# A hybrid attention step on one core: the successor operand loaded by a job, read-backs on another queue, states loaded at another place

## The chip, the core and the metric

The program runs on one core of a Trainium2 chip. TensorE (PE in the profile) multiplies, ScalarE (ACT) and VectorE (DVE) evacuate and transform, GpSimd (POOL) selects and issues DMAs, SyncE (SP) issues DMAs only. Each engine works through its own instructions in order; an instruction that waits holds up all that stand behind it on its engine, and that holds for DMA issues too. SP, ACT and POOL each have such a DMA queue here. The metric is the device time of one execution in microseconds: 2400.34 us is the median of three runs of the kernel before (2395.4 to 2400.91).

## What is computed

One layer of a hybrid streaming encoder for 1024 prompt frames and 8 x 16 sample frames, width 2048, in float32. Cut to what matters:

```python
h = rms_norm(x, norm_pre)
q_sb,k_sb,v_sb,g_sb, q_r,k_r,v_r,g_r = split(h @ w_in)      # 8 blocks of 8 heads x 128
# branch A: stick-breaking attention, strictly causal; sample rows also see 1024 cached keys and values
z = q k^T / sqrt(128);  a = sigmoid(z) * cumprod of sigmoid(-z) over the later keys;  o_sb = a v
# branch B: retention with a decay per head; the state s of 128 x 128 runs over the frames
o_r = (q k^T * decay) v + (q s) * decay;   s = s * decay + k^T v
y = concat(head_rms_norm(o_sb) * silu(g_sb), head_rms_norm(o_r) * silu(g_r)) @ w_out
x = x + rms_norm(y, norm_post)
```

It also returns the new keys and values, and the retention states of the prompt and of the eight sample streams.

## The kernel before, in words

**Tiling.** Frames are cut into tiles of 128. There are two groups: group 0 has the prompt tiles 0 to 3 and the sample tile (640 columns), group 1 the prompt tiles 4 to 7 (512 columns). The normalised, transposed input of a group is the moving operand `mov`: 16 strips (k = 0 to 15) of 128 rows in four blocks of four, each strip split into a high part `mh` (a rounded copy, ScalarE, line 131) and a low part `ml` (the rest, VectorE, line 132). Every product is then three matmuls, high by high, high by low and low by high. There is one set of SBUF blocks for `mov`; group 1 takes the place of group 0 block by block, once the products that read a block are issued.

**Loops.** For each group and each of 8 heads the kernel projects six columns of w_in (`project`, line 243: q, k and gate of both branches; four chunks of weights, each a DMA `wr`, line 215, a split into `wh` and `wl`, and the matmuls of line 229), and for each pair of heads the two value columns (`project_rows`, DMA line 271, matmuls line 288, tile names `wrn`, `whn`, `wln`, `accn`). Weight tiles `wr`, `wh`, `wl` have four buffers each.

**Jobs.** Around these products run jobs, Python generators stepped by `tick()`, which is called once after each product; a job that yields n comes again n ticks later. Jobs are the two branches of a head (`ret_branch`, `sb_branch`) and in group 0 the decoding of the sample tile (`decode`). The numbers after the yields (D_RET, D_TO, D_TI and so on, one for group 0 and one for group 1) place their instructions among the products. A planner then gives each engine its order by its own estimate of when things are ready. `tied` holds an instruction, in group 0, behind the product issued last; it orders the plan and adds no wait on the chip.

**Turning a tile.** A 128 x 128 transpose is done by writing the tile to DRAM (`turn_out`, line 471), reading it back with 32 x 32 blocks rearranged (`turn_in`, line 477: four DMAs, line 481), and transposing the blocks on VectorE. The reading back goes to the SP queue for the retention keys (`ro<-s_rk`), for the outputs of both branches (`ro<-s_o`, `so<-s_o`, `do<-s_o`) and for the decoder's weights (`be<-s_bd`); only the attention weights of the prompt (`kb<-s_be`, `be<-s_be`) are read back on GpSimd's queue.

**The change of groups.** The last head of group 0 (h = 7) ends with `project_pair` (line 249), which works on two gate columns together. `load_moving` (line 198) runs along with it: four strips of group 1 at each of its chunks 1, 2 and 3, and the last four in the first `project_rows` of group 1. A strip is a DMA `mr<-s_h` on SP's queue into one of two buffers, and the split. The prompt keys of group 1's first attention, `kpast` (line 962), use the same two buffers afterwards.

**Other loads touched.** `keys_out` stores the new keys (`out<-kn`, lines 869 and 874) from ScalarE's queue: 4 DMAs per head, and 4 more where the sample tile is in the group. `sample_retention` (line 802) loads the eight stored states of a head in four DMAs (`st<-state_ret`, line 808, SP) right where it starts, at the end of the head's retention. `retention` (line 747) begins with the decay table `dT` (line 749, SP).

Of the kernel before, what the change touches and what calls it, by code (L numbers as in the profile page):

```python
# [9 lines left out]
F32 = mybir.dt.float32  # L10
# [6 lines left out]
P = 128  # L17
D = 2048
KT = D // P
# [29 lines left out]
D_TI = (32, 13)  # L49
D_OUT = 4  # L50
D_KL = 29
D_TK = 4
D_FIN = 4
D_MR = 6
# [6 lines left out]
def tile_hybrid_step(  # L61
# [136 lines left out]
    def load_moving(mov, at, n, src, stage=None):  # L198
        hi, lo = mov
        for k in range(KT):  # L200
# [7 lines left out]
            split(hi[q][:, j, at : at + n], lo[q][:, j, at : at + n], r)  # L208
            yield D_MR

    def load_w(col):
        hs, ls = [], []
        for w in range(KT // WQ):
            wr = wp.tile([P, WQ, P], F32, name="wr", tag="wr")
            nc.sync.dma_start(
                wr,
                w_in[0, w * WQ * P : (w + 1) * WQ * P, col : col + P].rearrange("(k p) e -> p k e", p=P),
            )
# [30 lines left out]
    def project_pair(g, mov, cols, loads=None):  # L249

        accs = [acc_banks(g) for _ in cols]
        chunks = [load_w(c) for c in cols]
        for w in range(KT // WQ):
            for i, (acc, chunk) in enumerate(zip(accs, chunks)):
                _, wh, wl = next(chunk)
                for _ in range(WQ if loads and w and i == 0 else 0):
                    next(loads)
                products(mov, acc, g["pieces"], w, wh, wl)
        return [list(zip(acc, g["pieces"])) for acc in accs]

    col = lambda i, h: i * H * P + h * P

    def project_rows(g, mov, col, dst, off, loads=None):
        hi, lo = mov
        nt = len(g["tiles"])
        banks = [
            accp.tile([P, 2, 2 * P], F32, name=f"accn{b}", tag=f"acc{b % 2}") for b in range((nt + 1) // 2)
        ]
        for w in range(KT // 2):
            wr = wp.tile([P, 2, 2 * P], F32, name="wrn", tag="wr")  # L270
            nc.sync.dma_start(
                wr,
                w_in[0, 2 * w * P : 2 * (w + 1) * P, col : col + 2 * P].rearrange("(k p) e -> p k e", p=P),
            )
            for _ in range(WQ if loads and w == 0 else 0):
                next(loads)
            wh = wp.tile([P, 2, 2 * P], F32R, name="whn", tag="wh")
            wl = wp.tile([P, 2, 2 * P], F32R, name="wln", tag="wl")
            split(wh, wl, wr)
            for j in range(2):  # L280
                q, jj = divmod(2 * w + j, WQ)
                for t in range(nt):
                    a = banks[t // 2][:, t % 2, :]
                    ts = slice(t * P, (t + 1) * P)
                    for n, (lhs, rhs) in enumerate(((hi, wh), (hi, wl), (lo, wh))):


                        anchor[0] = nc.tensor.matmul(  # L288
                            a,
                            lhs[q][:, jj, ts],  # L290
                            rhs[:, j, :],
                            start=(w == 0 and j == 0 and n == 0 and t % 2 == 0),
                            stop=(w == KT // 2 - 1 and j == 1 and n == 2 and (t % 2 == 1 or t == nt - 1)),
                        )
                    tick()
        for b, bank in enumerate(banks):
            m = min(2, nt - 2 * b)
            nc.scalar.activation(
                dst[:, off + 2 * b : off + 2 * b + m].rearrange("p t j d -> p t (j d)"), bank[:, :m, :], AF.Copy
            )  # L300

    with ExitStack() as s1:
# [171 lines left out]
            q.dma_start(s.rearrange("k q c -> q k c"), src)  # L474
            return s

        def turn_in(s, raw, q):

            for i in range(4):
                tied(  # L480
                    q.dma_start(  # L481
                        raw[32 * i : 32 * i + 32, :].rearrange("p (k a) -> p k a", a=32),
                        s[:, :, 32 * i : 32 * i + 32].rearrange("k (j b) a -> b (k j) a", b=32),
                    )
                )
# [44 lines left out]
        class Out:  # L530
# [9 lines left out]
            def finish(self, b, h, gT, oT, dst):  # L540
# [4 lines left out]
                s = turn_out(self.o, f"s_o{b}_{h}_{self.nt}_{phase[0]}")  # L545
                yield D_TO[phase[0]]
                flat = self.o.rearrange("p k d -> p (k d)")
                turn_in(s, flat, nc.sync)
                yield D_TI[phase[0]]
                n = self.nt * P  # L550
                tied(nc.vector.transpose(oT[:, :n], flat))
# [73 lines left out]
        def decode(h, qs, rest):  # L625
# [81 lines left out]
            for _ in range(2):  # L707
                values.append(load_v(len(values)))
                yield D_TO[phase[0]] // 2
            turn_in(turned, be, nc.sync)  # L710
            for _ in range(V_BUFS - 4):
                values.append(load_v(len(values)))
                yield D_TI[phase[0]] // 2
# [33 lines left out]
        def retention(gi, g, h, out, rq, rk, rkn, rv):  # L747
# [8 lines left out]
                nc.vector.tensor_tensor(sc, ps[:, :P], dT[:, kind, :], ALU.mult)  # L756
                return sc

            S = None
            if gi == 1:  # L760
                S = op.tile([P, P], F32, name="S", tag="S", bufs=3)
                nc.sync.dma_start(S, s_S[h])
# [34 lines left out]
                yield D_RET[phase[0]]  # L797
            nc.scalar.dma_start(s_S[h] if gi == 0 else s_prompt[0, 0, h], S)
            if SAMPLE in g["tiles"]:
                yield from sample_retention(h, out, sc, rq, rkn, rv)  # L800

        def sample_retention(h, out, sc, rq, rkn, rv):
            i = 4

            sts = []
            for c in range(4):
                st = ip.tile([P, 2, P], F32, name="st", tag="st", bufs=4)
                tied(nc.sync.dma_start(st, state_ret[0, 2 * c : 2 * c + 2, h].rearrange("b d e -> d b e")))
                sts.append(st)
            yield 2 * D_RET[phase[0]]  # L810
            po = acc_tile()
            nc.tensor.matmul(po[:, 2 * P : 3 * P], sc, rv[:, i, :], start=True, stop=True)
# [28 lines left out]
        def ret_branch(gi, g, h, rq, rk, rv, rest):  # L841
# [19 lines left out]
        def sb_branch(gi, g, h, out, q2, k2, kT, rest):  # L861
            tiles, nt = g["tiles"], len(g["tiles"])
            off = 0 if gi == 0 else 4
            def keys_out():
                kn = ep.tile([P, nt * P], F32, name="kn", tag="rkn")
                nc.vector.transpose(kn, kT[:, : nt * P])
                for i in range(4):
                    q, ds = slice(32 * i, 32 * i + 32), slice(32 * i, 32 * i + 32)
                    nc.scalar.dma_start(
                        k_prompt[0, 0, tiles[0] * P : (tiles[0] + 4) * P, h, ds].rearrange("(j b) a -> b j a", b=32),  # L870
                        kn[q, : 4 * P].rearrange("p (j a) -> p j a", a=32),
                    )
                    if SAMPLE in tiles:
                        nc.scalar.dma_start(
                            k_sample[0].rearrange("b t h d -> (b t) h d")[:, h, ds].rearrange("(j b) a -> b j a", b=32),
                            kn[q, 4 * P :].rearrange("p (j a) -> p j a", a=32),
                        )
                yield 1
# [16 lines left out]
        for gi, g in enumerate(GROUPS):  # L895
# [7 lines left out]
            for h in range(H):  # L903
# [328 lines left out]
```

## Time and profile before

| | |
|---|---|
| median of three runs | 2400.34 us |
| the profiled execution | 2397.79 us |
| its span, first to last instruction | 2396.1 us |
| mean granted TensorE clock | 0.993 |
| group 0 | to about 1120 us |
| change of groups | about 1080 to 1230 us |
| group 1 | from about 1130 to about 2000 us |
| output projection | from about 1963 us |

The profile is one execution on the chip. Its page gives busy time by engine, the chain of work that ended last, and the costliest groups; other views give the busy time of each engine in chosen stretches, who waited for whom, one tile's instructions, and the instructions in order of time. A line such as `L215` is a line of the kernel before; `wr<-w_in` names output and input tile. `SPq` and `ACTq` are DMA issues on those queues, with the time that the issue took, not the transfer. PEclk is the clock that TensorE was granted, as a share of the full one. What stands in square brackets at the end of a timeline row is the engine's idle time before the instruction, and what ended it.

### The profile page before, as it was taken

What the parts mean: (1) busy time and instruction counts of PE and PEld (TensorE: products, weight loads), DVE (VectorE), ACT (ScalarE), POOL (GpSimd) and SP (SyncE); (2) the same over time, 40 slices, a digit from 0 to 9 for tenths busy, and PEclk for the clock granted to TensorE, in tenths of its full rate; (3) what the DMA queues carried; (4) which work ended last, traced back from release to release, by engine and by line L of the source; (5) the groups of instructions that cost most, each with busy time, mean ns of one, the idle gap of its engine ahead of it and who ended that gap; (6) DMA issues with size and microseconds to landing.
All of it is one profiled execution on the core that took longest, in us unless ns stands there. A gap on an engine that the chain in (4) does not pass through costs nothing.

```text
span 2396.1 us, 40529 instructions
## 1 busy us (share of the span) xinstructions
PE 2332.6 (97%) x14832; PEld 2094.6 (87%) x14832; DVE 1254.6 (52%) x2442; ACT 919.6 (38%) x1937; POOL 646.2 (27%) x1033
## 2 busy tenths in 40 slices
PE   7999999999999999998899999999999999999998
PEld 7998899999999999987778888889898888888887
DVE  7245455445554555455545554555554566564544
ACT  6323333324333333324333343343343444444443
POOL 3144353444344353443302111120220220010000
PEclk9999999999999999999999999999999999999999
DMA  7658879797889879798875555556654667765553
GB/s 244 166 130 210 167 166 197 174 199 164 188 178 191 181 174 187 182 192 199 188 189 150 150 141 150 146 142 153 153 152 127 166 163 195 231 214 181 189 191 131
DMA packets 677050, 418.68 MB, mean 175 GB/s; under 512 B 224753, under 2 KB 620017, under 8 KB 674545
## 3 DMA queue, kind: packets, MB, share of 16 engines
q1 hardware_dynamic: 524272, 285.99, 47.6%
q0 software_dynamic: 32256, 71.36, 13.7%
q10 hardware_dynamic: 120320, 58.74, 9.0%
q8 instruction: 116, 1.90, 0.3%
q14 instruction: 86, 0.70, 0.1%
HBM read 336.24 MB, written 79.69 MB: 174 GB/s over the span
## 4 chain that ended last, share of the span: by engine, by line
PE 83%; DMA 7%; DVE 4%; issue 2%; ACT 2%; SPq 1%; POOL 0%; DVEq 0%; ACTq 0%; POOLq 0%
PE acc L229 44%; PE accn L288 17%; DMA mr<-s_y 4%; PE a L1031 3%; PE a L1032 3%; PE a L1030 3%; PE pa L618 3%; PE z L588 2%; DMA wr<-w_in 2%; PE zc L661 1%; PE pd L728 1%; DMA mr<-s_h 1%; DVE wl L132 1%; DVE ml L132 1%; ACT mh L131 1%
## 5 line engine op out<-in xcount | busy, mean ns | idle before, releaser
L229 PE MATMUL acc<-mh,wh 128*128 128x256 f32 (+2 forms) x2304 | 665.4, 342 | 7.8 <-ACT wh L131 5.0
L132 DVE TENSOR_TENSOR wl<-wr,wh 128x512 fp32r<-128x512 f32 (+1 forms) x576 | 391.8, 685 | 523.8 <-ACT wh L131 513.8
L229 PE MATMUL acc<-ml,wh 128*128 128x384 f32 (+2 forms) x2304 | 663.8, 341 | 0.0
L229 PE MATMUL acc<-mh,wl 128*128 128x256 f32 (+2 forms) x2304 | 660.2, 339 | 0.6 <-DVE wl L132 0.5
L131 ACT ACTIVATE wh<-wr 128x512 fp32r<-128x512 f32 (+1 forms) x576 | 357.4, 625 | 730.9 <-PE acc L229 247.7
L229 PEld LDWEIGHTS acc<-mh,wh 128*128 128x128 f32 x2304 | 420.7, 189 | 45.0 <-ACT wh L131 7.1
L229 PEld LDWEIGHTS acc<-mh,wl 128*128 128x128 f32 x2304 | 424.7, 189 | 31.6 <-issue 2.1
L229 PEld LDWEIGHTS acc<-ml,wh 128*128 128x128 f32 x2304 | 422.9, 189 | 33.2 <-issue 5.3
L645 POOL DMA_DIRECT2D kc<-cache_sb_k x512 | 331.6, 653 | 370.0 <-DVE kcT L683 205.9
L288 PE MATMUL accn<-whn,mh 128*128 128x256 f32 x1152 | 329.2, 287 | 0.6 <-ACT whn L131 0.5
L288 PE MATMUL accn<-wln,mh 128*128 128x256 f32 x1152 | 325.9, 283 | 1.5 <-DVE wln L132 1.5
L288 PE MATMUL accn<-whn,ml 128*128 128x256 f32 x1152 | 325.9, 283 | 0.0
L288 PEld LDWEIGHTS accn<-whn,mh 128*128 128x128 f32 x1152 | 220.5, 192 | 10.5 <-issue 7.5
L288 PEld LDWEIGHTS accn<-wln,mh 128*128 128x128 f32 x1152 | 220.9, 192 | 2.5 <-DVE wln L132 1.7
L288 PEld LDWEIGHTS accn<-whn,ml 128*128 128x128 f32 x1152 | 220.9, 192 | 0.0
L1031 PE MATMUL a<-wl,mh 128*128 128x512 f32 (+1 forms) x576 | 219.5, 381 | 0.2 <-DVE wl L132 0.2
L1032 PE MATMUL a<-wh,ml 128*128 128x512 f32 (+1 forms) x576 | 219.0, 381 | 0.0
L1030 PE MATMUL a<-wh,mh 128*128 128x512 f32 (+1 forms) x576 | 218.9, 381 | 0.0
L132 DVE TENSOR_TENSOR wln<-wrn,whn 128x512 fp32r<-128x512 f32 x128 | 87.5, 687 | 119.7 <-ACT whn L131 119.5
L131 ACT ACTIVATE whn<-wrn 128x512 fp32r<-128x512 f32 x128 | 80.1, 633 | 151.6 <-PE accn L288 65.4
L481 POOL DMA_DIRECT2D be<-s_be x128 | 94.0, 741 | 134.2 <-DMA s_be<-be 114.6
L1031 PEld LDWEIGHTS a<-wl,mh 128*128 128x128 f32 x576 | 108.4, 188 | 21.2 <-DVE wl L132 0.9
(189 smaller groups left out, 2611.6 us busy)
## 6 DMA issues: line engine op xcount, KB each, us to landing
wr<-w_in SPq DMA_DIRECT2D x384, 256.0 KB, 4.2
wr<-w_out SPq DMA_DIRECT2D x184, 256.0 KB, 3.6
wrn<-w_in SPq DMA_DIRECT2D x128, 256.0 KB, 3.2
kc<-cache_sb_k POOLq DMA_DIRECT2D x512, 64.0 KB, 4.6
vc<-cache_sb_v SPq DMA_DIRECT2D x64, 512.0 KB, 8.5
xt<-x_prompt SPq DMA_DIRECT2D x8, 1024.0 KB, 6.2
xr<-x_prompt SPq DMA_DIRECT2D x8, 1024.0 KB, 6.5
out<-out ACTq DMA_DIRECT2D x24, 256.0 KB, 3.6
```

The lines of the kernel that those rows point to most:

```text
L131: nc.scalar.activation(hi, src, AF.Copy)
L132: nc.vector.tensor_tensor(lo, src, hi.bitcast(F32), ALU.subtract)
L229: last = nc.tensor.matmul(a[:, :m], lhs[:, j, :], rhs[w][:, j, o : o + m], start=(w == 0 and j == 0 and n == 0), stop=(w == KT // WQ - 1 a ...
L288: anchor[0] = nc.tensor.matmul(a, lhs[q][:, jj, ts], rhs[:, j, :], start=(w == 0 and j == 0 and n == 0 and t % 2 == 0), stop=(w == KT // 2 ...
L481: q.dma_start(raw[32 * i : 32 * i + 32, :].rearrange("p (k a) -> p k a", a=32), s[:, :, 32 * i : 32 * i + 32].rearrange("k (j b) a -> b (k ...
L588: nc.tensor.matmul(z[:, :c], q2[a][:, i * P : (i + 1) * P], k2[b][:, s : s + c], start=(m == 0), stop=(m == 2),)
L618: nc.tensor.matmul(po[:, :P], at[:, j, :], vn[:, j, :], start=(j == 0), stop=(j == t))
L645: nc.gpsimd.dma_start(kc[32 * i : 32 * i + 32, :].rearrange("p (k d) -> p k d", d=32), cache_k[0, 2 * c + j, s * 512 : (s + 1) * 512, h, 3 ...
L661: mm = nc.tensor.matmul(z[r, :], qp[:, j, r], ready[2 * j + c // 2][:, c % 2, :], start=(j == 0), stop=(j == 1),)
L1030: nc.tensor.matmul(a[:, :width], hi[q][:, j, ts], wh, start=(k == 0), stop=False)
L1031: nc.tensor.matmul(a[:, :width], hi[q][:, j, ts], wl, start=False, stop=False)
L1032: nc.tensor.matmul(a[:, :width], lo[q][:, j, ts], wh, start=False, stop=(k == KT - 1))
```

## The change

Four things.

1. At the change from group 0 to group 1 the strips are loaded by a job of its own, the class `Successor`, stepped by `tick()` like the others. It asks for a strip every 5 ticks (D_NX) once the old block may be overwritten (`read`, set by `project_pair`), with the DMA on ScalarE's queue and tied to the products, and puts a strip (the split) one step after its DMA was asked for, so two are held. `project_rows` waits, by ticking, until the strip that it is about to read has been put. The change from group 1 to the output projection keeps `load_moving`.
2. From that point on `turn_in` reads back through `back[0]`, which is set to GpSimd's queue: this takes the last read-backs of group 0's head 7 and all of group 1's.
3. From that point on the key stores go to the same queue, out of ScalarE's.
4. In every head of group 0 the four state loads are issued at the start of `retention`, behind `dT`, and no longer in `sample_retention`.

```diff
+D_NX = 5
+    class Successor:
+        def __init__(self, n, src):
+            self.mov, self.n, self.src = [[], []], n, src
+            self.read, self.ready = 0, 0
+            self.job = Job(self.steps(), 1)
+
+        def steps(self):
+            held = []
+
+            def put():
+                k, r = held.pop(0)
+                q, j = divmod(k, WQ)
+                split(self.mov[0][q][:, j, : self.n], self.mov[1][q][:, j, : self.n], r)
+                self.ready = k + 1
+
+            for k in range(KT):
+                q, j = divmod(k, WQ)
+                while self.read <= q:
+                    yield 1
+                if j == 0:
+                    for x, y in zip(self.mov, moving_part(mp, NMAX, q)):
+                        x.append(y)
+                r = wp.tile([P, self.n], F32, name="mr", tag="mr", bufs=2)
+                tied(nc.scalar.dma_start(r, self.src(k)))
+                held.append((k, r))
+                yield D_NX
+                if len(held) == 2:
+                    put()
+            while held:
+                put()
+                yield 2
+
+        def wait(self, k):
+            while self.ready <= k:
+                tick()
 # project_pair
-                for _ in range(WQ if loads and w and i == 0 else 0):
-                    next(loads)
+                if isinstance(loads, Successor):
+                    loads.read = w
+                else:
+                    for _ in range(WQ if loads and w and i == 0 else 0):
+                        next(loads)
                 products(mov, acc, g["pieces"], w, wh, wl)
+        if isinstance(loads, Successor):
+            loads.read = KT // WQ
 # project_rows
-            for _ in range(WQ if loads and w == 0 else 0):
-                next(loads)
...
             for j in range(2):
+                if loads:
+                    loads.wait(2 * w + j)
 # turn_in, its callers, and keys_out
+        back = [nc.sync]
-        def turn_in(s, raw, q):
+        def turn_in(s, raw, q=None):
+            q = q or back[0]
-                turn_in(s, flat, nc.sync)
+                turn_in(s, flat)
-            turn_in(turned, be, nc.sync)
+            turn_in(turned, be)
-            turn_in(s, raw, nc.sync)
+            turn_in(s, raw)
+                store = nc.scalar if back[0] is nc.sync else back[0]
-                    nc.scalar.dma_start(
+                    store.dma_start(
 # retention and sample_retention
-            S = None
+            S, sts = None, []
+            if SAMPLE in g["tiles"]:
+                for c in range(4):
+                    st = ip.tile([P, 2, P], F32, name="st", tag="st", bufs=4)
+                    tied(nc.sync.dma_start(st, state_ret[0, 2 * c : 2 * c + 2, h].rearrange("b d e -> d b e")))
+                    sts.append(st)
-            sts = []
-            for c in range(4):
-                st = ip.tile([P, 2, P], F32, name="st", tag="st", bufs=4)
-                tied(nc.sync.dma_start(st, state_ret[0, 2 * c : 2 * c + 2, h].rearrange("b d e -> d b e")))
-                sts.append(st)
 # gates, last head of group 0
-                    after = [[], []]
-                    loads = load_moving(after, 0, *((NB_TOK, from_h), (3 * P, from_y, (ip, 6)))[gi])
+                    if gi == 0:
+                        back[0] = nc.gpsimd
+                        loads = Successor(NB_TOK, from_h)
+                        after = loads.mov
+                    else:
+                        after = [[], []]
+                        loads = load_moving(after, 0, 3 * P, from_y, (ip, 6))
```

In the changed program's instruction order all 16 strip loads stand on ScalarE's queue among the activations of head 7; 29 read-backs of four DMAs each and 40 key stores have moved to GpSimd's; and in each of the heads 1 to 7 of group 0 a part of the retention's small matmuls, which before alternate with 18 or more products at a time, stand together in front of the first products that follow the state loads.

More of the change, by code (lines that the diff above doesn't have):

```diff
@@ L799, in retention, with sample_retention @@
             if SAMPLE in g["tiles"]:
-                yield from sample_retention(h, out, sc, rq, rkn, rv)
-        def sample_retention(h, out, sc, rq, rkn, rv):
+                yield from sample_retention(h, out, sc, rq, rkn, rv, sts)
+        def sample_retention(h, out, sc, rq, rkn, rv, sts):
             i = 4
-            sts = []
-            for c in range(4):
-                st = ip.tile([P, 2, P], F32, name="st", tag="st", bufs=4)
-                tied(nc.sync.dma_start(st, state_ret[0, 2 * c : 2 * c + 2, h].rearrange("b d e -> d b e")))
-                sts.append(st)
             yield 2 * D_RET[phase[0]]
@@ L873, in keys_out @@
                     if SAMPLE in tiles:
-                        nc.scalar.dma_start(
+                        store.dma_start(
                             k_sample[0].rearrange("b t h d -> (b t) h d")[:, h, ds].rearrange("(j b) a -> b j a", b=32),
```

## The prediction

> **What bounds the kernel now.** First the page:
>
> ```profile
> span 2396.1 us, 40529 instructions
> PE 2332.6 (97%) x14832; PEld 2094.6 (87%) x14832; DVE 1254.6 (52%) x2442; ACT 919.6 (38%) x1937; POOL 646.2 (27%) x1033
> PE 83%; DMA 7%; DVE 4%; issue 2%; ACT 2%; SPq 1%; POOL 0%; DVEq 0%; ACTq 0%; POOLq 0%
> ```
>
> TensorE is busy 2332.6 of 2396.1 us: a change that keeps the products can win only part of the 63.5 us left, and its clock losses. So I asked for the busy time by stage; below are the end of group 0 with group 1's first products, group 1's first projections, and one and a half heads behind them (us, busy time and count by engine, clock, DMA share, GB/s).
>
> ```profile
> 1080.00:1145.00 65.00, 56.11 (x374) 49.58 (x374) 37.90 (x87) 29.98 (x67) 26.02 (x45) 0.95 0.80 195
> 1145.00:1230.00 85.00, 75.86 (x435) 60.52 (x434) 40.59 (x79) 27.52 (x57) 13.98 (x24) 0.94 0.82 189
> 1230.00:1354.00 124.00, 122.94 (x679) 106.88 (x678) 65.07 (x122) 47.32 (x99) 19.15 (x30) 1.00 0.59 155
> ```
>
> The change of groups loses 8.9 + 9.1 = 18.0 us of idle TensorE in 150 us, the next 124 us only 1.1. Its clock is low too: (1 - 0.95) x 65 + (1 - 0.94) x 85 = 8.4 us of full-speed time at most, since part of that lies in the idle time. The ceiling is 18.0 - 1.3 (the later rate over 150 us) + 8.4 = 25 us, 1%. Next, whom TensorE waits for between 1060 and 1260:
>
> ```profile
> PE acc L229 <- ACT wh L131: 4.7, 1, 4.7
> PE zc L661 <- DVE kcT L683: 4.1, 1, 4.1
> PE pSs L832 <- DVE st L835: 2.7, 1, 2.7
> PE pa L815 <- DMA st<-state_ret: 2.4, 1, 2.4
> ```
>
> The strips (of 1060 to 1260, and of the whole span):
>
> ```profile
> L132 DVE TENSOR_TENSOR ml<-mr,mh x16: 646/691/778, 1094.5 to 1140.5; 128x512 fp32r<-128x512 f32 x16
> L207 SPq DMA_DIRECT2D mr<-s_h x14: 319/320/344, 1095.2 to 1135.8; - x14
>   DMA mr<-s_h: 17.3, 10
>   DMA out<-kn: 5.0, 1
> DMA to landing us min/median/max: 2.4/4.4/6.0
> ...
> L207 SPq DMA_DIRECT2D mr<-s_h x16: 319/323/497, 104.8 to 1135.8; - x16
> ```
>
> Two strips were fetched at about 105 us; the other 14 go through two buffers in seven rounds, 1095.2 to 1141.2, 6.6 us a round. ScalarE stands 17.3 us in front of them, and 5.0 us behind key stores. VectorE, in order, stands behind ScalarE, and with it the state update that `pSs` waits for. The chain of waits shows where that ends, and the SP queue what comes after:
>
> ```profile
> 1142.89 14.42 PE accn L288 x118
> 1157.31 2.75 PE acc L229 x12
> ...
> 1164.33 9.37 DMA wr<-w_in
> ...
> 1198.51 1.42 SPq L689 DMA_DIRECT2D vc<-cache_sb_v  x1
> 1200.10 4.78 SPq L481 DMA_DIRECT2D so<-s_o  x4
> 1204.92 2.17 SPq L481 DMA_DIRECT2D ro<-s_rk  x4
> 1208.81 1.14 SPq L689 DMA_DIRECT2D vc<-cache_sb_v  x2
> 1209.99 7.20 SPq L215 DMA_DIRECT2D wr<-w_in  x4
> 1219.82 0.79 PE L229 MATMUL acc<-mh,wh 128*128 128x512 f32 x1 [4.68 <-ACT wh L131]
> ```
>
> Weights are asked for at 1209.99 only, behind two read-backs and the decoder's values; TensorE waits 4.68 us for them. The 4.1 us of `zc` are of the same kind: VectorE stands in front of a late `wr`, the one of 1164.33, 9.37 us under way.
>
> **The parts.** The sum is made against the profiled execution's 2397.8 us (span 2396.1); the median of the runs shown is 2400.3, 2.5 us above it.
>
> *Strips by a job: -8.* What it gives is the point at which the first `project_rows` of group 1 is through, 1157.31 now. The loads still go through two buffers, and all 16 now start at the change, since they are tied: eight rounds for seven. They start where the first split stands now, about 1093.5. A round of landing 4.4, split by ScalarE and VectorE (0.63 + 0.69; ScalarE's 128x512 form is near VectorE's 0.691) is 5.7 us, so the last strip is ready at 1093.5 + 8 x 5.7 = 1139; at the present 6.6 us a round it is 1146. The strip loads now stand in order among ScalarE's activations, and each waits for VectorE's split of two strips before, so I take the slow round. Behind the last strip only two strips' products are left, 2 x 12 x 14.42/118 = 2.9 us, where now 118 matmuls are: 1149, 8 us earlier. The fast round gives 1142 and would be 15, but idle time and clock there allow 8.9 + 3.3 = 12. The other end is 0: the products creep behind the strips with gaps of their own. In this stage the 2.4 us of `st` and the 5.0 us of ScalarE behind `kn` go too; both are within the 12, not on top. Queued behind a strip load on ScalarE are weight splits, which have time while TensorE still works on earlier chunks.
>
> The clock is the reason why gaps count for more than their length:
>
> ```profile
> 1110.00:1120.00 10.00, 7.62 (x41) 5.04 (x39) 5.43 (x11) 4.56 (x10) 7.94 (x14) 0.83 1.02 248
> 1170.00:1180.00 10.00, 5.85 (x25) 2.56 (x18) 5.08 (x8) 4.50 (x9) 0.89 (x4) 0.76 0.62 163
> ```
>
> A gap of 2.4 us at 1111 costs 1.7 us of clock, one of 4.1 at 1171 costs 2.4. By the Trainium skill, "TensorE: Matmul & The Clock Gate", section "What's actually happening", the clock falls to half only after an idle window of about 3.4 us and comes back after a busy one. The trace has it falling around a shorter gap; by the page's rule creeping products with gaps near 1.5 us would keep full speed and the term would stay at -8, by the row some of them may pay.
>
> *Read-backs and key stores off SP and ScalarE: -8 at the change, +2 in group 1.* At the change the wait of 4.7 us loses its cause, and the 4.1 us probably, since SP then holds weights, values and `kpast` only: with the clock 5.1 us, 9.1 + 5.1 = 14.2 us are to be had. The values remain, so I take 8; the lower end is 3, where weights stay late behind them. GpSimd pays in group 1:
>
> ```profile
> L481 POOL DMA_DIRECT2D be<-s_be x128: 682/745/808, 1258.2 to 1990.8; - x128
> L481 SPq DMA_DIRECT2D ro<-s_o x64: 302/487/3123, 190.7 to 1996.1; - x64
> PE pa L618 <- DVE kp L578: 5.0, 6, 1.1
> POOL be L481 <- DMA s_be<-be: 105.0, 28, 6.5
> ```
>
> A head of group 1 gets 12 read-backs and 4 stores, 16 x 0.745 = 11.9 us on an engine that is busy 19.15 of 124 us: there is room. But a read-back may stand behind one that waits for its DRAM write (105.0/28 = 3.8 us each), its transpose on VectorE comes later, and TensorE already waits 5.0 us in group 1 (1240 to 1900) for transposed weights. Bounds: -5, all of that idle time; +26, each of 24 read-backs costs the longest of these waits, 1.1. I take +2, near the low end, as the six waits are the only rows in which TensorE feels these tiles.
>
> *States asked for early: +2.* The load's issue and landing, then the stretch in which it now goes, heads 1 and 2:
>
> ```profile
> L808 SPq DMA_DIRECT2D st<-state_ret x28: 367/510/692, 293.5 to 1109.9; - x28
> ...
> 261.43 2.87 SPq L749 DMA_DIRECT2D dT<-c_dt  x1
> 264.35 14.26 SPq L215 DMA_DIRECT2D wr<-w_in  x9
> 260.00:270.00 10.00, 6.41 (x47) 5.08 (x46) 5.36 (x15) 0.87 (x3) 5.89 (x9) 0.87 1.02 169
> ...
> 398.73 1.25 SPq L749 DMA_DIRECT2D dT<-c_dt  x1
> 400.08 2.04 SPq L215 DMA_DIRECT2D wr<-w_in  x4
> 406.13 0.63 ACT L131 ACTIVATE wh<-wr 128x512 fp32r<-128x512 f32 x1 [0.78 <-DMA wr<-w_in]
> 408.89 0.46 PE L229 MATMUL acc<-mh,wh 128*128 128x256 f32 x2
> PE pa L772 <- DVE sc L756: 0.8, 2, 0.4
> ```
>
> Four loads go between `dT` and the weights: 4 x 0.51 = 2.0 us of SP, or by bytes 0.5 MB at 0.19 MB a us = 2.8. In head 2 the weights' split ends at 406.76 and is used at 408.89: 2.1 us of slack, so the stall is 0 to 0.7. The program's order has retention matmuls stand in that place, which fill 1 us or so of it. Head 1 has no slack, TensorE idles there already: +1. I take the five others as head 2. The last row is the longest of TensorE's waits in 300 to 1060: the stage has nothing to win. Ends: 0, and 7 x (2.8 + 1.7 of clock) = 31.5.
>
> Sum: -8 - 8 + 2 + 2 = -12; 2397.8 - 12 = **2386 us**.
>
> **Rivals.** *A: the strips pace the change anyway.* Two buffers and eight rounds leave 1157 where it is, and the values keep the weights late: 0 - 3 + 4 gives 2399. For it: the round hardly gets shorter. Against: key stores and SP's other work leave the rounds.
>
> *B, slower: the state loads hold the weights in every head.* One place, behind `dT` in heads 1 to 7, at up to 4.5 us each: -16 + 2 + 31.5 = +17.5, 2415. It decides from 14/7 = 2.0 us a head on. For it: the planner has the retention stand together there, as if it expected the wait, and `dT` once took 2.87. Against: 2.1 us of slack.
>
> *C: the whole ceiling comes back*, 25 us, and GpSimd and states cost nothing: 2373. For it: each of the four waits has its cause touched. Against: TensorE follows the strips.
>
> *D, slower: GpSimd's DMA issue is held up by VectorE.* VectorE is busy 65.07 of 124 us in group 1; if the 24 read-backs come late by that, at the 26 us above: -16 + 26 + 2 = +12, 2410. Against: GpSimd's 128 issues there take 0.682 to 0.808, as even as could be. This is the Trainium skill's rule in "SBUF — State Buffer", section "SBUF: two separate sides": while VectorE holds the shared ports in its two-port modes, GpSimd can't write descriptors. The trace doesn't show such a hold.
>
> **How the numbers follow.** Forecast 0.58, A 0.14, B 0.09, C 0.14, D 0.05. A measurement of this kernel tells about 0.3% (7 us) from none. Faster: most of the forecast (0.53), C, and 0.03 of A: 0.70. Same: the rest of A and 0.04 of the forecast: 0.15; slower: B, D and 0.01: 0.15. The likeliest case's own range is 2376 to 2396; 2370 to 2404 takes in C in part and A, and leaves out B and D.
>
> **What would show it.** Right: TensorE idle and clock loss in the 150 us of the change down from 18 + 8 to about 10; the first `acc` of group 1 near 1149; no wait of `acc` for `wh` over 3 us behind it; heads 2 to 7 of group 0 as long as now. Wrong: ScalarE's idle time before `mh` above 17.3 us with the same 1157 (A); new TensorE waits at the first chunk behind `dT` with a low clock (B); GpSimd issues above 0.81 us or longer waits of `pa` for `kp` in group 1 (D).

## The result, and the profile after

The changed kernel takes 2412.01 us in the median of six runs (2407.57 to 2416.09), the kernel before beside it 2398.02 (2395.4 to 2404.21): 1.0062 times as long, 95% interval 1.0051 to 1.0073. The change makes the kernel slower by 0.6%, where 2386 us were forecast. Its profiled execution is the shortest of its runs, 2407.57 us; the profile therefore shows 9.5 us of the 14 us between the medians, in its span:

```profile
span 2405.6 us, 40512 instructions
PE 2338.4 (97%) x14832; PEld 2093.5 (87%) x14832; DVE 1251.7 (52%) x2442; ACT 910.6 (38%) x1931; POOL 749.9 (31%) x1189
```

TensorE has the same 14832 matmuls. The busy time of the three stretches at the change of groups (us, busy time and count by engine, clock, DMA share, GB/s), and whom TensorE waited for between 1060 and 1260:

```profile
1080.00:1145.00 65.00, 58.35 (x401) 51.58 (x394) 40.38 (x95) 32.28 (x72) 31.44 (x55) 0.95 0.83 205
1145.00:1230.00 85.00, 78.74 (x431) 66.18 (x433) 43.49 (x81) 27.44 (x59) 28.64 (x48) 0.96 0.88 192
1230.00:1354.00 124.00, 119.77 (x696) 102.11 (x689) 64.33 (x121) 46.73 (x98) 36.18 (x55) 0.97 0.62 162
```

```profile
PE pa L662 <- DVE kb L622: 6.2, 1, 6.2
PE pd L772 <- DMA vc<-cache_sb_v: 4.2, 1, 4.2
PE zc L705 <- DVE st L878: 2.2, 1, 2.2
PE accn L330 <- DVE wln L133: 1.5, 1, 1.5
```

The four waits of the kernel before (of `acc` for `wh` 4.7, `zc` for `kcT` 4.1, `pSs` for `st` 2.7, `pa` for `st` from memory 2.4) are gone from the head of the list; `zc` now waits 2.2 for VectorE's work on `st`. TensorE's idle time in the first two stretches falls from 18.0 to 12.9 us. Two new waits stand in their place, 6.2 and 4.2 us, the second in the third stretch, where the idle time rises from 1.1 to 4.2 us and the clock falls from 1.00 to 0.97.

Idle time alone leaves out the half clock and work that the planner put elsewhere. So I count each matmul with the median distance to the next one among those of its tiles and width in the trace of before; what a stage takes beyond the sum of its matmuls is its loss. A stage ends at the start of the same product of `project` in every trace; "strips" ends with group 1's first one, which the whole of the first `project_rows` precedes, "heads 2 to 7" begins at 408.9 us in the trace of before, and "tail" is all from the start of group 1's last chunk of `project` to the last matmul.

| loss in us | start | heads 2 to 7 of group 0 | end of group 0, strips | behind the strips | group 1 | tail |
|---|---|---|---|---|---|---|
| stage ends in the trace of before | 408.9 | 1077.6 | 1157.2 | 1264.7 | 1984.6 | 2396.1 |
| before | 41.0 | 51.5 | 18.0 | 21.3 | 14.7 | 0.9 |
| changed | 39.4 | 59.2 | 12.8 | 21.4 | 15.8 | 7.7 |
| only states early | 41.9 | 59.3 | 14.4 | 18.7 | 14.6 | 0.5 |
| only the job | 43.8 | 51.3 | 21.1 | 22.3 | 13.7 | 1.8 |
| only the queues | 44.7 | 52.0 | 12.3 | 17.2 | 16.2 | 7.2 |
| job and queues | 41.1 | 51.4 | 16.2 | 21.9 | 16.6 | 5.1 |
| the same, strips on SP | 41.4 | 52.2 | 12.8 | 17.0 | 17.3 | 5.1 |
| queues only in the change | 43.1 | 51.4 | 15.4 | 14.9 | 13.0 | 0.4 |

(The rows from the third on are experiments below.) The change wins 5.2 us up to the strips, nothing behind them, loses 7.7 us in heads 2 to 7 and 6.8 us in the tail, where nothing was expected. In all kernels with late states TensorE has the same order of matmuls up to 1120 us, and still the column "start" lies between 39.0 and 45.7 us over their traces: single executions differ by that much, and the medians decide on the sum, the table on the place.

*Where the first new wait comes from.* GpSimd's instructions in order (start, duration, and in brackets its idle time and what ended it), then VectorE's:

```profile
1167.47 0.79 POOL L516 DMA_DIRECT2D s_be<-kb  x1 [0.27 <-issue]
1194.04 1.32 POOL L525 DMA_DIRECT2D ro<-s_rk  x2 [25.79 <-DMA s_rk<-rk]
1195.35 0.65 POOL L525 DMA_DIRECT2D kb<-s_be  x1
...
1197.09 1.94 POOL L525 DMA_DIRECT2D kb<-s_be  x3
```

```profile
1207.41 0.71 DVE L622 STREAM_TRANSPOSE kb<-kb 128x512 f32<-128x512 f32 x1 [4.04 <-DMA kb<-s_be]
```

The scores of group 0's last row are written out at 1167.47. Their read-back `kb<-s_be`, which was on GpSimd's queue already, stands behind `ro<-s_rk`, which the change put there and which waits until 1194.04 for a store that ScalarE issued at 1185.34. GpSimd stands 25.79 us with other work behind it, VectorE stands for the read-back, and TensorE for VectorE. But `ro<-s_rk` is not alone in front of it. Three of the read-back's four DMAs also stand behind decoding's selects (L550 and L556, 1196.01 to 1197.09), and the sigmoids that these work on end on ScalarE at 1193.78, only 0.26 us before GpSimd is released:

```profile
1193.48 0.30 ACT L545 ACTIVATE be<-zn 128x128 f32<-128x128 f32 x1
```

By these times the selects would have held the three DMAs until 1193.8 without `ro<-s_rk` too; `back_first_sp` below tries it with the strips on SP. In the kernel before, the selects ran at 1179.11. TensorE's products `zc`, from which the sigmoids are made, stood 57 matmuls behind group 1's first product there, and stand 147 behind it now; why the planner puts them later was not taken apart.

*The strips* (1060 to 1260), and the first product behind them:

```profile
L235 ACTq DMA_DIRECT2D mr<-s_h x16: 326/327/452, 1097.9 to 1142.5; - x16
L133 DVE TENSOR_TENSOR ml<-mr,mh x16: 648/692/693, 1101.7 to 1147.0; 128x512 fp32r<-128x512 f32 x16
  DMA mr<-s_h: 16.5, 10
```

```profile
1157.94 0.40 PE L266 MATMUL acc<-mh,wh 128*128 128x512 f32 x1
```

The last strip is split at 1147.0 + 0.7 = 1147.7, the first product comes at 1157.94, with `project_rows` in between (1147.7 to 1157.9):

```profile
L330 PE MATMUL accn<-whn,mh 128*128 128x256 f32 x29 | 8.2, 283 | 0.0
L330 PE MATMUL accn<-wln,mh 128*128 128x256 f32 x29 | 8.2, 283 | 0.0
L330 PE MATMUL accn<-whn,ml 128*128 128x256 f32 x29 | 8.2, 283 | 0.0
```

None of these matmuls waits for a strip. `project_rows` has 192 of them, twelve to a strip in the order of the strips; the last twelve start at 1156.5, 8.8 us after the split that they need, and for the other strips the distance is longer. In the trace of before the last strip is ready at 1141.2 and its twelve start at 1155.7; the shortest distance there is 13.7 us. Over all sixteen traces it is 6.3 us, and none of them has a wait of TensorE for `mh` or `ml` between 1060 and 1260.

*The tail.* TensorE's waits from 1940 to 2250, and the rows of VectorE and ScalarE at the first:

```profile
PE pa L821 <- DVE sc L800: 4.2, 1, 4.2
PE a L1080 <- DVE wl L133: 1.4, 5, 0.5
PE a L1079 <- ACT wh L132: 1.1, 2, 0.8
```

```profile
1973.36 0.43 DVE L133 TENSOR_TENSOR ml<-mr,mh 128x256 fp32r<-128x256 f32 x1 [6.59 <-ACT mh L132]
1973.70 0.29 DVE L800 TENSOR_TENSOR sc<-rs,dT 128x128 f32<-128x128 f32 x1
```

```profile
1972.91 0.42 ACT L132 ACTIVATE mh<-mr 128x256 fp32r<-128x256 f32 x1 [5.09 <-DMA mr<-s_y]
```

The retention's score `sc` of the last head stands on VectorE behind a piece of the next operand, which stands on ScalarE for its load. Before, the longest wait of TensorE in this stretch was 1.1 us.

### The profile page after: what moved, and what is told of

The parts are those of the page before. It is cut to its first block, busy times and chain, and to the rows that moved or that the text cites. A ratio compares the mean times of both kernels' runs of the same rounds, so it can differ in the third digit from the quotient of the medians.

```text
span 2405.6 us, 40512 instructions
## 1 busy us (share of the span) xinstructions
PE 2338.4 (97%) x14832; PEld 2093.5 (87%) x14832; DVE 1251.7 (52%) x2442; ACT 910.6 (38%) x1931; POOL 749.9 (31%) x1189
```

## The experiments

Times are medians, ratios are to runs of the kernel before on the same chip. "On GpSimd" always means from the change of groups on.

### Each part alone, and the two queue parts together

The first three are the kernel before with one part each; `job_back` is the changed kernel with the states where they were:

```diff
 # states_only: the early st loads alone, in retention (SP)
 # job_only: Successor and loads.wait alone
 # back_only: back[0] = nc.gpsimd alone, with the old load_moving
 # job_back: changed kernel, and
-            S, sts = None, []
-            if SAMPLE in g["tiles"]:
-                for c in range(4): ... sts.append(st)
+            S = None
```

> The kernel before with one part of the change alone: the states of decoding asked for ahead of the retention of a head instead of behind it. Theory 1 (the loss of the change sits on GpSimd's queue, in the change of groups): the seven heads of group 0 lose about 5 us behind dT, as in the trace of the change, and the eighth gives them back, so 2396 to 2402 us. Rival 2 (state loads hold up the weights and are the loss): 2406 us or more. Rival 3 (the job of strips is the loss): as the kernel before, 2396 to 2400 us.

2400.25 us, 1.0011 (1.0000 to 1.0022), in the range of theory 1.

> The kernel before with the job alone: strips of the new operand on ScalarE's queue, read-backs on SP, key stores on ScalarE, states late. Theory 1: the strips set the same pace, so the first product behind them starts near 1157 us; what SP's read-backs cost behind it (gaps of 4.5 and 4.9 us in the kernel before) stays: 2394 to 2402 us. Rival 2: as the kernel before. Rival 3: the strips and splits on ScalarE come between its other work, 2406 us or more.

2406.1 us, 1.0034 (1.0022 to 1.0045), in the range of rival 3.

> The kernel before with the moved queues alone: from the change of groups on, read-backs and key stores on GpSimd's queue; strips on SP as before, states late. Theory 1: the gaps behind SP's read-backs go (about 10 us won), and a wait of pa for VectorE's transposes and of pd for vc, with GpSimd standing behind a read-back, takes as much or more, and the tail loses some 8 us: 2404 to 2412 us. Rivals 2 and 3: the queues are a gain, 2386 to 2394 us.

2399.6 us, 1.0007 (0.9994 to 1.0019), between the two expectations: both miss.

> The changed kernel with the states late, as in the kernel before. Theory 1: the loss stays, 2404 to 2414 us. Rival 2: the loss goes with the early states, 2388 to 2398 us. Rival 3: it stays too; the job alone tells it from theory 1.

2407.57 us, 1.0038 (1.0026 to 1.0051): the loss stays in the larger part, as theory 1 had it.

My theory after the result, that the loss sits on GpSimd's queue, falls in part: the queues alone cost next to nothing, and the job alone, which I had put at nothing, costs 0.34%. The table of losses says where. The queues do win what the prediction saw at the change (5.7 us up to the strips, 4.1 behind them) and give back 6.3 us in the tail. The job turns those gains round: beside the queues it costs 16.2 - 12.3 = 3.9 us at the strips and 21.9 - 17.2 = 4.7 us behind them. Early states cost 7.8 us in heads 2 to 7 and give back 3.6 us at the end of group 0 and 2.6 us behind the strips. SP shows what stands in front of the weights (kernel with early states alone):

```profile
533.54 0.84 SPq L793 DMA_DIRECT2D dT<-c_dt  x1
534.43 1.99 SPq L807 DMA_DIRECT2D st<-state_ret  x4
536.47 10.54 SPq L252 DMA_DIRECT2D wr<-w_in  x5
```

Four state loads, 1.99 us of SP's time, go between `dT` and the weights. That is about half of the loss: TensorE's idle time in heads 2 to 7, between the same products as in the table, rises from 2.9 to 6.6 us. The other 4 of the 7.8 us are in matmuls that take longer in the new order, 3.0 us in the retention's small ones (`rs`, `pS`, `pa` from the state), which now stand together, and 1.7 us in `zc`, against small gains in others.

### The job's queue, the key stores, the head of GpSimd's line, the tail

```diff
 # job_sp: job_back, and
-                tied(nc.scalar.dma_start(r, self.src(k)))
+                tied(nc.sync.dma_start(r, self.src(k)))
 # back_reads: back_only, and
-                store = nc.scalar if back[0] is nc.sync else back[0]
+                store = nc.scalar
 # back_first_sp: back_only, and in ret_branch
-            turn_in(s, raw)
+            turn_in(s, raw, nc.sync if (gi, h) == (1, 0) else None)
 # back_tail_sp: back_only, and at the head of the loop over h
+                if gi == 1 and h == H - 2:
+                    back[0] = nc.sync
```

> The changed kernel with the states late and the job's strips issued on SP's queue instead of ScalarE's. Theory 4 (the job loses because its strips are issued in ScalarE's order, behind ScalarE's own work: the last strip was issued at 1145.4 us with the job alone, at 1135.8 us before): the loss of the job goes, 2396 to 2402 us, as with the moved queues alone. Rival 5 (it loses by the job's pace, two strips held and a wait of five ticks for each, whatever the queue): 2404 to 2412 us, as with strips on ScalarE.

2396.23 us, 1.0000 (0.9991 to 1.0009), against 1.0038 with the strips on ScalarE. The job's pace is not what costs; the queue is, with the order that follows from it. The strips' rows, first with ScalarE's queue (`job_back`), then with SP's (`job_sp`):

```profile
L235 ACTq DMA_DIRECT2D mr<-s_h x16: 326/327/1712, 1092.9 to 1139.8; - x16
L133 DVE TENSOR_TENSOR ml<-mr,mh x16: 648/692/755, 1096.6 to 1146.1; 128x512 fp32r<-128x512 f32 x16
  DMA mr<-s_h: 21.0, 10
```

```profile
L235 SPq DMA_DIRECT2D mr<-s_h x16: 319/338/1071, 1091.6 to 1137.2; - x16
L133 DVE TENSOR_TENSOR ml<-mr,mh x16: 683/691/694, 1097.7 to 1142.1; 128x512 fp32r<-128x512 f32 x16
  DMA mr<-s_h: 17.3, 9
```

On SP the first split is 1.1 us later and the last 4.0 us earlier. A load in ScalarE's order comes when ScalarE comes to it: between two of its strip loads, at 1127.7 and 1135.2, ScalarE had other work and waits of its own. But TensorE waits for no strip, so a later strip is not yet a loss. The loss goes the other way: a strip load on ScalarE waits for VectorE's split of two strips before, and ScalarE's other work stands behind it. The kernel with the job alone shows it most plainly, in two waits of TensorE and in ScalarE's rows in front of them:

```profile
PE z L632 <- ACT be L545: 2.6, 1, 2.6
PE accn L330 <- ACT whn L132: 2.6, 1, 2.6
```

```profile
1138.26 0.35 ACTq L235 DMA_DIRECT2D mr<-s_h  x1
1138.65 0.60 ACT L545 ACTIVATE be<-zc 128x512 f32<-128x512 f32 x1 [1.50 <-DVE ml L133]
...
1141.29 0.34 ACTq L235 DMA_DIRECT2D mr<-s_h  x1
1141.68 0.63 ACT L132 ACTIVATE mh<-mr 128x512 fp32r<-128x512 f32 x1 [1.15 <-DVE ml L133]
1142.21 1.13 ACT L132 ACTIVATE whn<-wrn 128x512 fp32r<-128x512 f32 x2
```

In `job_back` the wait for `whn` is 1.3 us; with the strips on SP there is none above 0.2 for weights from 1080 to 1160. These waits are a part of the difference; the rest of it was not followed wait by wait.

> Read-backs alone on GpSimd's queue from the change of groups on; the key stores stay on ScalarE. Theory 1 (the read-backs win at the change and lose in the tail; the key stores do little): within 4 us of the kernel with both moved, 2395 to 2404 us. Rival (the key stores, eight issues of 0.65 us each ahead of the cache loads of decode, make the decode chain late and so the wait for vc): 2390 to 2395 us.

2412.13 us, 1.0066 (1.0053 to 1.0079): both expectations miss. Key stores left on ScalarE while the read-backs go by GpSimd cost 0.6% against moving both; the loss in group 1 is 22.8 us instead of 16.2, at the strips 19.5 instead of 12.3. Beside the moved read-backs, the key stores' move is a gain of the change; alone it was not run.

> Read-backs and key stores on GpSimd's queue alone (strips on SP, states late), with one exception: the four read-backs of the retention keys of group 1's first head stay on SP. With them on GpSimd's queue its trace shows GpSimd idle for 16.15 us behind them at 1184.76 us, and VectorE's transpose then late by 3.7 us for the scores' read-back behind. Theory 1 (head of the line on GpSimd's queue): that gap of pa (3.25 us and a half clock behind it) goes, the chain of decode comes earlier and the wait of pd for vc (4.37 us) shrinks, so group 1 is reached some 5 to 11 us earlier and the time is 2389 to 2396 us. Rival (the scores' read-back would be late anyway, as in the kernel with the job alone, where it comes 6.8 us late behind SP's read-backs): the wait returns at the same place, 2397 to 2404 us.

2401.6 us, 1.0016 (1.0006 to 1.0025), in the rival's range. The retention keys are off GpSimd's line, and the wait of `pa` only falls from 3.1 to 2.5 us, for another instruction holds the read-back up (GpSimd in order; the L550 are decoding's selects, which want ScalarE's sigmoids):

```profile
1169.85 1.32 POOL L525 DMA_DIRECT2D kb<-s_be  x2 [3.30 <-DMA s_be<-kb]
1193.40 0.29 POOL L550 TENSOR_SCALAR_AFFINE_SELECT kp<-kp 128x128 f32<-128x128 f32 x1 [22.23 <-ACT kp L544]
```

Two of the read-back's four DMAs stand in front of that wait and two behind it, so the transpose has to wait for it all the same.

> Read-backs and key stores on GpSimd's queue from the change of groups on, but back on SP and ScalarE from group 1's seventh head on. Theory 1: what is lost behind the last projection (9.6 us between the last projection's chunk and the end, against the kernel before) is due to the read-backs on GpSimd in the last heads, and goes: 2386 to 2394 us. Rival (the loss comes from the order in which the planner put the output projection, whatever the queue): it stays, 2396 to 2403 us.

2393.07 us, 0.9985 (0.9977 to 0.9994), against 1.0007 without the return to SP: theory 1. The loss of the tail falls from 7.2 to 2.4 us, that of group 1 from 16.2 to 11.0. TensorE's longest wait from 1940 to 2250, without the return (`back_only`) and with it (`back_tail_sp`):

```profile
PE pa L816 <- DVE sc L800: 4.9, 1, 4.9
```

```profile
PE pa L662 <- DVE ro L825: 1.5, 1, 1.5
```

### The changed kernel with parts undone

The same edits, on the changed kernel; `both_undone` has strips on SP, the return to SP in the seventh head and late states, `both_undone_early` the same with early states.

> The changed kernel with one thing undone: the job's strips go by SP's queue again. Theory 4 (the strips' place on ScalarE is the larger part of the loss; 9 us of medians lay between the two queues with the states late): 2399 to 2405 us, group 1 reached some 5 to 8 us earlier than in the changed kernel. Rival (the strips' queue matters only with the states late): 2408 us or more.

2405.66 us, 1.0037 (1.0024 to 1.0050), 0.7 us above the range of theory 4 and below the rival's.

> The changed kernel with one thing undone: from group 1's seventh head on the read-backs go by SP's queue and the key stores by ScalarE's again. Theory 1 (the changed kernel loses some 10 us behind its last projection by the read-backs on GpSimd's queue): 2400 to 2406 us, with no wait of pa for sc above 2 us behind 1940 us and no loss between the last projection and the end. Rival (what is won there is not won in the changed kernel, since its order of the last heads is another): 2408 us or more.

2403.8 us, 1.0027 (1.0017 to 1.0036), in the range of theory 1.

> Strips of the job by SP's queue, read-backs and key stores on GpSimd's queue from the change of groups to group 1's sixth head and on SP and ScalarE behind it, states late. If the two losses are separate, their gains add: group 1 reached near 8.7 us ahead of the kernel before and no loss behind it, 2386 to 2391 us. If they overlap: 2392 to 2396 us, as with the better one of them alone.

2392.95 us, 0.9982 (0.9971 to 0.9992). The gains do not add: this is no better than the return alone (0.9985).

> As the kernel with both undone, but with the states asked for early, as in the changed kernel. Theory 1 (early states lose in heads two to seven of group 0 what the eighth gives back): within 3 us of that kernel. Rival 2 (early states cost the 4 us that lay between the changed kernel and the one with late states): 3 to 6 us above it.

2397.04 us, 1.0003 (0.9989 to 1.0018), 0.21% above the same with late states: rival 2, though the two intervals touch.

These give the change's loss step by step: from 0.9982 early states go to 1.0003, strips on ScalarE to 1.0027, GpSimd's queue in the last two heads to 1.0062. Of 2397 us that is +5.0, +5.8 and +8.4 us on -4.3, the 14.9 of the result. By the intervals each step is uncertain by 3 to 4 us, and in another order the steps would have other sizes. The early states' price in other pairs is 2.6 us (alone), 5.8 (changed kernel against `job_back`) and 8.9 (`after_strips_sp` against `job_sp`): uneven, always a loss, larger than what the profiles show of it.

### What holds the stage behind the strips, and a better version

```diff
 # kb_sp: back_tail_sp, and in read_back (group 0's last row of scores)
-                        turn_in(turned, be, nc.gpsimd)
+                        last = (todo[0][1], h, step) == (0, H - 1, 4)
+                        turn_in(turned, be, nc.sync if last else nc.gpsimd)
 # back_change: back_only, and at the head of the loop over h
+                if gi == 1 and h == 1:
+                    back[0] = nc.sync
```

> Read-backs and key stores on GpSimd's queue from the change of groups to group 1's sixth head, states late, strips on SP by the old loop; and the scores' last read-back of group 0 (kb<-s_be of the eighth head) goes by SP's queue. Theory 6 (this read-back is late since GpSimd comes to it only behind decoding's selects, which stood 22.23 us at 1193.40 us for ScalarE's sigmoids in the kernel with the retention keys on SP): the wait of pa for VectorE's transpose near 1202 us (3.79 us in that kernel without the step) goes, group 1 is reached 2 to 5 us earlier, 2388 to 2392 us. Rival (SP brings it late too, behind the weight loads that stand there, or the next wait, of pd for vc, takes what is won): the same as without the step, 2391 to 2396 us.

2391.31 us, 0.9974 (0.9964 to 0.9985), a time that both ranges hold. The wait of `pa` is gone, so the order on GpSimd's queue was its cause. Group 1 is not reached earlier (the stage behind the strips loses 16.1 us instead of 17.6), because the chain of decoding is late and TensorE meets it at the next place (waits from 1190 to 1260):

```profile
PE pd L765 <- DVE kp L759: 3.9, 1, 3.9
PE pd L773 <- DMA vc<-cache_sb_v: 2.5, 1, 2.5
```

> Read-backs and key stores on GpSimd's queue only from the change of groups to the end of group 1's first head, then on SP and ScalarE again; states late, strips on SP by the old loop. Theory 1 (the gain lies at the change, the rest of group 1 does not care, the loss lies in the last heads): as with the return in the seventh head, 2390 to 2396 us. Rival (SP's read-backs cost group 1 something in its second to sixth head, as the prediction of the change took for the queue moved the other way): 2397 us or more.

2388.86 us, 0.9961 (0.9949 to 0.9973): the fastest, ahead of both kernels and 1.1 us below the range of theory 1. It has neither job nor early states; read-backs and key stores are on GpSimd from the change to the end of group 1's first head, on SP and ScalarE elsewhere.

```profile
1080.00:1145.00 65.00, 57.67 (x395) 51.00 (x394) 39.11 (x88) 30.84 (x69) 29.16 (x51) 0.95 0.82 199
1145.00:1230.00 85.00, 82.97 (x486) 69.26 (x486) 45.38 (x85) 28.62 (x63) 30.28 (x50) 0.98 0.83 192
```

TensorE's idle time in these two stretches is 9.4 us, where it was 18.0, and the clock of the second is 0.98 instead of 0.94.

## Why the prediction was wrong

*The ceiling and the stage* were right. The loss was at the change of groups, SP's read-backs held weights up, and taking them away in just that stage gives the gain: 8.6 us less idle time in `back_change`.

*Strips by a job, -8: this step failed, in its sign.* With late states the choice of queue is worth 0.38% (9 us) against the job; in the changed kernel 0.25% (6 us). The reckoning of the last strip held: 1147.7 us, on 1146 taken. What failed is the premise that TensorE follows the strips. In the sum it has the form "behind the last strip only two strips' products are left": the three groups of 29 above were left, 87 matmuls and not 24, and the first product of group 1 came at 1157.94, not at 1149. The prediction's own lines of the kernel before, with 118 matmuls behind 1142.89 and the last split done at 1141.2, already had the strips ahead of TensorE. No trace has a wait for a strip, so an earlier last strip had nothing to give by itself; what the strips can hold up is the work behind them on ScalarE and VectorE. The 1157 of rival A came, but A's mechanism, that the strips pace the change, is not in the traces either. ScalarE's wait in front of the strips, 16.5 us of 17.3, hardly fell.

The cost was put at nothing with the words that the weight splits behind a strip load "have time while TensorE still works on earlier chunks". With the job alone TensorE waits 2.6 us for such a split and 2.6 us for a sigmoid that stands behind a strip load too. On SP's queue the same job costs nothing: 1.0000, on 1.0007 without it.

Behind the strips the changed kernel loses 21.4 us, as before, where the queues alone lose 17.2. One difference is visible there. In the three kernels with the read-backs on GpSimd and the strips on ScalarE, SP issues two loads of `vc` (0.5 MB each) 2.1 to 2.6 us before ScalarE stores `s_rk` (the two rows below are SP's and ScalarE's in the changed kernel), and GpSimd is released 8.2 to 9.5 us after that store's issue. In the eight with strips on SP and both stores and read-backs on GpSimd, SP issues them later than the store, by 1.1 to 4.0 us, and the release comes 3.0 us behind it. That the values' bytes are what delays the store fits, and was not tried by itself.

```profile
1182.74 1.12 SPq L733 DMA_DIRECT2D vc<-cache_sb_v  x2
```

```profile
1185.34 0.38 ACTq L516 DMA_DIRECT2D s_rk<-rk  x1
```

The late store doesn't explain the stage, though. An earlier release only lets GpSimd stand for the sigmoids instead (8.78 us in `back_only`): from group 1's first product to the transpose of `kb` pass 49.5 us in the changed kernel and 50.7 in `back_only`. TensorE's wait is longer in the changed kernel since it comes to `pa` sooner, 44.1 us and 208 matmuls behind that product, not 48.4 us and 227. And `after_strips_sp`, where the release comes after 3.0 us, loses 21.3 us behind the strips as well. What makes up the difference in this stage stays open.

*Read-backs and key stores, -8 at the change.* The size was right (5.7 + 4.1 = 9.8 us alone), the wait it named went (no `acc` waits over 3 us for `wh`), and the key stores were part of it. What the prediction didn't see is the order on the queue that they went to: `ro<-s_rk` and decoding's selects ahead of `kb<-s_be`. It knew that "a read-back may stand behind one that waits for its DRAM write", but charged it to group 1 alone, at 1.1 us at most each; at the change TensorE's wait for that read-back is 3.1 us with the queues alone and 6.2 in the changed kernel. *+2 in group 1* was right in its size: 1.1 us more loss in the trace, and the waits for the scores' transposes did not grow (1240 to 1900):

```profile
PE pa L662 <- DVE kp L622: 3.4, 4, 1.1
L525 POOL DMA_DIRECT2D be<-s_be x124: 685/740/802, 1264.2 to 1972.0; - x124
```

The second row, of 1250 to 2000, is against rival D: GpSimd's issues take 0.685 to 0.802 us, as before, beside a busy VectorE. The rule of the Trainium skill behind D ("SBUF — State Buffer", section "SBUF: two separate sides"), which holds for VectorE in its two-port modes, would show as longer issues, and no run here shows them.

*The tail has no term in the sum.* The change moves the queue until the end; the prediction followed it only to 1900 us. Behind that, eight or so microseconds were lost, by the medians of the undone step. The wait of 4.2 us for `sc` and those at `wr` in the output projection are what the trace shows of it; why the planner's order of the last heads gives them with one queue and not with the other was not taken apart.

*States early, +2.* The direction was right and the size too small: 5.0 us in the step above. In the trace heads 2 to 7 lose 7.7 us more, 1.3 us a head; with early states alone it is 7.8, of which 3.6 come back when the states are no longer waited for in the last head. Rival B had a part of the mechanism, weights that wait behind the states; the longer matmuls of the new order were in neither. B counted on more than 2.0 us a head for the time to turn; it needed less, since the other gains were not there. *The range*, 2370 to 2404, was exceeded by 8 us because the job and the tail had no loss in it at all.

## What to carry to other kernels

Before a load is moved so that it comes earlier, find the wait that ends with it: compare the time at which each piece is ready with the time of its first use. Here the strips were ready 13.7 us or more ahead, and loading them earlier had nothing to win by itself. When DMA issues move to another in-order queue, write down that queue's order around the move, with what each entry waits for, up to the end of the program; a read-back that waits 25 us for its store, or a load that waits for another engine, holds everything behind it. A queue that helps in one stage can be given back behind it: here the move limited to the change was worth 0.39%, the same move kept to the end nothing.

## What the runs showed of the hardware

The clock fell around short gaps once more. In the changed kernel TensorE's longest wait between 1110 and 1140 is the 2.2 us of `zc`, from 1125.9 to 1128.05, and these are the two stretches around it:

```profile
1120.00:1130.00 10.00, 6.67 (x44) 4.48 (x46) 7.40 (x19) 6.21 (x12) 2.59 (x5) 0.86 0.61 154
1130.00:1140.00 10.00, 9.29 (x57) 7.33 (x49) 4.43 (x10) 5.31 (x11) 9.32 (x17) 0.80 0.82 205
```

The clock is 0.86 and then 0.80, with TensorE busy 9.29 of 10 us in the second. The rule of the Trainium skill in "TensorE: Matmul & The Clock Gate", section "What's actually happening", an idle window of about 3.4 us, would leave the full clock here; the trace decides against it, as the gap of 2.4 us did before. The other observation is the spread at the start: the same matmuls in the same order lost 39.0 to 45.7 us in the first 400 us of single executions, and 51.3 to 52.3 in the six heads that follow.
